# Recurrent gates in split precision, stored weight splits spread over the FFN, shared score banks, and three reorderings in a two-layer flow step

## The chip, the cores and the metric

The kernel runs on one core of one Trainium2 chip. The metric is the device time of one execution in microseconds (us): the median of the runs shown. TensorE (PE) multiplies matrices, VectorE (DVE) and ScalarE (ACT) do elementwise work, GpSimd (POOL) does a little elementwise work and issues part of the DMAs, SyncE (SP) issues most of the other DMAs. Each engine works through its own list of instructions in order.

## The reference

One inference step of two layers over 512 latent tokens and 128 context tokens, D = 1024, all in float32. Layer 0 mixes tokens by neighbourhood attention (16 heads of 64; the context tokens attend to themselves), layer 1 by a bidirectional gated linear recurrence. A SwiGLU FFN of width 2816 follows each. Every sublayer has a modulated RMS norm in front and a gated residual behind. The part that changes most, the recurrence, is cut here:

```python
def _lru_mixer(xm, h0, w_in, conv_w, conv_b, w_a, b_a, w_i, b_i, lam, w_out):
    gate, xr = jnp.split(xm @ w_in, 2, axis=-1)
    xc = _centred_depthwise_conv(xr, conv_w, conv_b)                  # width 4
    # per direction, with block-diagonal 128x128 weights (8 blocks):
    #   r = sigmoid(xc @ w_a + b_a);  i = sigmoid(xc @ w_i + b_i)
    #   a = exp(-8 r softplus(-lam)); b = sqrt(1 - a^2) * (i * xc)
    #   h_t = a_t h_{t-1} + b_t, from cached states for latent tokens
    y = (hs_f + hs_b) * jax.nn.gelu(gate)
    return y @ w_out, ...

def _swiglu(x, w_gu, w_down):
    gate, up = jnp.split(x @ w_gu, 2, axis=-1)
    return (jax.nn.silu(gate) * up) @ w_down
```

## The kernel before, in words

Everything is kept transposed: 128 features on the partitions, 640 tokens on the free axis, 8 such tiles ("KT") for D. A float32 product is done as three products of rounded parts: the operand is split into a high part (a cast to the fp32r type, on ACT) and a low part (the rest, by a subtraction on DVE), and `chunk` adds high x high, high x low and low x high for 8 tiles into one PSUM bank: 24 products of 320 or 322 columns. This is called a sum below. The split of a weight tile (`unit`, with `split` doing one ACT cast and one DVE subtraction) is done in the kernel. The recurrent gates are the exception: `gates` multiplies in full fp32, 512 and 131 columns for each gate, four gates per tile.

**Stored splits.** During the first FFN the kernel splits weights ahead of time for later stages: `keep` loads a raw tile through POOL's DMA queue, casts and subtracts it (behind the last evacuation, `mark`), and stores both parts in HBM, again through POOL's queue. Later `unit` loads both parts from there through SP's queue. `todo` lists the tiles: 16 of the recurrence's input weight "wi", 8 of its output weight "wlo", 5 of the second FFN's "gu". The raw tiles share three buffers ("mraw") with the modulation weights, whose products (`mod_cols`, "mprod") DVE does in small portions (`fill`) beside the sums.

**First FFN.** Three parts of 8, 7 and 7 hidden tiles (`ci` 0, 1, 2). For each tile j of a part come the gate and the up sums (four sums), then the part's down products (`project`, 16 sums). `keep` is called in the second and third part behind each tile, twice, up to the tile that `LATE` names, and in the first part's down products once for each output tile.

**Attention.** For each pair of heads p = 0..7 four blocks of 128 latent queries are done (`softmax`) and the prompt (`softmax_prompt`), in two halves, b0 = 0 and 2: scores on two "sp" banks, exp, a scaling by the reciprocal of the sum (one head on DVE, the other on ACT), transposes, and the products with V (`heads_out`). The output projection (`project` with `ahead`) comes behind, and its first sums can start before the last head's output is there, as far as banks are free.

**Recurrence.** `lru` runs a list `order` of steps with lags; one turn is called a lap, and there are 8, one for a tile f. On PE a lap has gates 0, 1, 2 of tile f, the sum `xa` of tile f+1 (its own bank "mx"), gate 3, then the sums `xb`, `ga` and `gb` (tags "mm", three banks in turn). `cv` (L1347, DVE) makes the convolution that the next lap's gates read. The program order of PE, DVE and ACT is held in this stage; elsewhere a planner chooses among the instructions that can run.

**Opening of the second FFN.** The recurrence's output weights are multiplied with y. Six banks (three output tiles, both halves) add up y's tiles 0 to 5, then 6, then 7; y's last tile comes late, because the last lap's scans have to end.

PSUM has eight banks: three "mm" banks that live throughout, and five that each stage lays out anew: attention tp 2, sp 2, op 1; first FFN at 2, rr 1, mx 2; recurrence mx 1 and two double banks "gp" for gates; second FFN at 1, mx 3, mc 1.

## Time and profile before

| | us |
|---|---|
| median of 3 runs | 1507.13 (1506.39 to 1509.18) |
| profiled execution | 1509.39 |
| its span in the trace | 1507.3 |
| PE busy in the span | 1477.6 (98%) |
| DVE busy | 1079.3 (72%) |
| ACT busy | 722.2 (48%) |
| POOL busy | 272.6 (18%) |

The profile is of one execution. "Busy" of PE is the time in which at least one product is under way; products overlap, so the pace of a stream is read from the distance of starts and not from the duration of one. A timeline row gives start, length, engine, line, operation and output<-inputs; a bracket at its end is how long the engine had been idle before it and what ended that. Tile names are those of the program: gp is a gate bank, xc the convolution's output, mx and mm are sum banks, whi/wlo and whx/wlx split weights.

### The profile page before, as it was taken

The page shows a single profiled execution, that of the slowest core. Times are in us where ns is not written, and L with a number is a line of the kernel's source. Part 1 is how long each engine was busy: PE and PEld are TensorE (multiplying, and loading weights), DVE is VectorE, ACT ScalarE, POOL GpSimd, SP SyncE. Part 2 cuts the span into 40 slices and gives each one's busy share as a digit, 9 for nine tenths or more (in the row PEclk, how much of TensorE's full clock was granted, in tenths as well). Part 3 has the DMA queues.
Part 4 walks back from the last instruction along what each step waited for, and adds up shares of the span by engine and source line. Part 5 has one row for each costly group of instructions (what it writes and reads, how often), then busy time and mean ns, then how long its engine had stood idle before and what let it go on. Part 6 is the DMA issues. An engine that isn't in the chain of part 4 may idle for free.

```text
span 1507.3 us, 26208 instructions
## 1 busy us (share of the span) xinstructions
PE 1477.6 (98%) x10305; PEld 1430.9 (95%) x10305; DVE 1079.3 (72%) x2034; ACT 722.2 (48%) x1336; POOL 272.6 (18%) x345
## 2 busy tenths in 40 slices
PE   7999999999999999999999999999999999999997
PEld 4999999889999999999999988899989999999997
DVE  5788887869964678888776478885875675565555
ACT  4676766664333324322443378863644342424244
POOL 0211121100100212211210001112123323222211
PEclk9999999999999999999999999999999999999999
DMA  9544645435532889886964633246332131313211
GB/s 374 170 149 148 186 148 157 124 140 181 183 126 71 304 292 327 307 271 211 324 244 138 236 126 126 71 165 225 118 124 88 67 112 57 112 57 98 71 57 70
DMA packets 83674, 246.99 MB, mean 164 GB/s; under 512 B 9264, under 2 KB 22752, under 8 KB 83424
## 3 DMA queue, kind: packets, MB, share of 16 engines
q1 hardware_dynamic: 58384, 154.97, 31.2%
q0 software_dynamic: 24848, 90.20, 17.4%
q8 instruction: 81, 1.33, 0.4%
q14 instruction: 41, 0.34, 0.1%
q10 hardware_dynamic: 320, 0.16, 0.0%
HBM read 202.02 MB, written 39.34 MB: 160 GB/s over the span
## 4 chain that ended last, share of the span: by engine, by line
PE 82%; DVE 6%; DMA 5%; issue 3%; ACT 3%; POOL 1%; SPq 0%; DVEq 0%; POOLq 0%; ACTq 0%
PE mm L246 12%; PE mm L247 12%; PE mm L245 12%; PE mx L245 4%; PE mx L247 4%; PE mx L246 4%; PE mx L1158 3%; PE mx L1159 3%; PE mx L1160 3%; PE gp L1364 2%; DMA mraw<-in_wm 2%; PE op L849 2%; PE tp L766 2%; PE mc L1158 1%; PE mc L1160 1%
## 5 line engine op out<-in xcount | busy, mean ns | idle before, releaser
L246 PE MATMUL mm<-big,whi 128*128 128x320 f32 (+2 forms) x1003 | 311.9, 311 | 2.2 <-DVE big L1470 2.2
L245 PE MATMUL mm<-big,whi 128*128 128x320 f32 (+2 forms) x1003 | 310.3, 312 | 2.3 <-ACT big L1469 1.4
L247 PE MATMUL mm<-big,wlo 128*128 128x320 f32 (+2 forms) x1003 | 311.6, 311 | 0.2 <-DVE wlo L1470 0.2
L284 DVE SCALAR_TENSOR_TENSOR mprod<-mraw,csb 128x1024 f32<-128x1024 f32 x160 | 195.6, 1223 | 19.1 <-DMA mraw<-in_wm 18.4
L246 PEld LDWEIGHTS mm<-big,whi 128*128 128x128 f32 x1003 | 189.6, 189 | 4.2 <-DVE big L1470 3.2
L245 PEld LDWEIGHTS mm<-big,whi 128*128 128x128 f32 x1003 | 188.9, 189 | 4.9 <-ACT big L1469 2.3
L247 PEld LDWEIGHTS mm<-big,wlo 128*128 128x128 f32 x1003 | 189.4, 189 | 1.6 <-DVE wlo L1470 0.4
L1469 ACT CAST whi<-raw 128x1024 fp32r<-128x1024 f32 (+2 forms) x103 | 105.5, 1025 | 152.3 <-PE mm L246 83.8
L1470 DVE TENSOR_TENSOR wlo<-raw,whi 128x1024 fp32r<-128x1024 f32 (+2 forms) x103 | 127.8, 1241 | 38.8 <-ACT whi L1469 38.3
L247 PE MATMUL mm<-big,wlx 128*128 128x320 f32 (+3 forms) x450 | 139.4, 310 | 0.0
L246 PE MATMUL mm<-big,whx 128*128 128x320 f32 (+3 forms) x450 | 139.3, 310 | 0.0
L245 PE MATMUL mm<-big,whx 128*128 128x320 f32 (+3 forms) x450 | 139.1, 309 | 0.0
L567 DVE SCALAR_TENSOR_TENSOR x<-mm,G,x 128x320 f32<-128x320 f32 (+3 forms) x207 | 83.1, 434 | 61.4 <-PE mm L247 53.6
L245 PE MATMUL mx<-big,whi 128*128 128x320 f32 (+2 forms) x325 | 101.7, 313 | 0.2 <-ACT whi L1469 0.2
L247 PE MATMUL mx<-big,wlo 128*128 128x320 f32 (+2 forms) x325 | 100.6, 310 | 0.0
L246 PE MATMUL mx<-big,whi 128*128 128x320 f32 (+2 forms) x325 | 100.5, 309 | 0.0
L280 POOL DMA_DIRECT2D mraw<-in_wm x80 | 43.2, 540 | 315.3 <-DVE mprod L284 205.4
L246 PEld LDWEIGHTS mm<-big,whx 128*128 128x128 f32 x450 | 84.9, 189 | 0.0
L247 PEld LDWEIGHTS mm<-big,wlx 128*128 128x128 f32 x450 | 84.9, 189 | 0.0
L245 PEld LDWEIGHTS mm<-big,whx 128*128 128x128 f32 x450 | 84.8, 188 | 0.0
L247 PE MATMUL mx<-big,wlx 128*128 128x320 f32 (+3 forms) x222 | 68.9, 310 | 0.0
L246 PE MATMUL mx<-big,whx 128*128 128x320 f32 (+3 forms) x222 | 68.9, 310 | 0.0
(375 smaller groups left out, 3835.9 us busy)
## 6 DMA issues: line engine op xcount, KB each, us to landing
raw<-in_gu SPq DMA_DIRECT2D x84, 512.0 KB, 3.7
mraw<-in_wm POOLq DMA_DIRECT2D x80, 512.0 KB, 4.5
raw<-in_dn SPq DMA_DIRECT2D x24, 512.0 KB, 3.6
raw<-in_wqk SPq DMA_DIRECT2D x16, 512.0 KB, 4.1
sw<-in_wm SPq DMA_DIRECT2D x16, 512.0 KB, 10.2
mraw<-in_wi POOLq DMA_DIRECT2D x16, 512.0 KB, 6.2
kwi<-kwh POOLq DMA_DIRECT2D x16, 512.0 KB, 5.7
kwi<-kwl POOLq DMA_DIRECT2D x16, 512.0 KB, 5.7
```

The lines of the kernel that those rows point to most:

```text
L245: nc.tensor.matmul(ps, hi[:, k], xhi[:, k, s], start=(k == 0), stop=False)
L246: nc.tensor.matmul(ps, hi[:, k], xlo[:, k, s], start=False, stop=False)
L247: nc.tensor.matmul(ps, lo[:, k], xhi[:, k, s], start=False, stop=(k == nk - 1))
L280: nc.gpsimd.dma_start(w, self.i["wm"][l * 6 + j - 2, f])
L284: nc.vector.scalar_tensor_tensor(prod, w, 1.0, self.csb[:, s], ALU.mult, ALU.mult, accum_out=out[:, s, f:f + 1])
L567: last = self.nc.vector.scalar_tensor_tensor(xs, ps[:, a - t0:b - t0], G[:, s, f:f + 1], xs, ALU.mult, ALU.add).ins
L766: nc.tensor.transpose(tp[:, j * P:j * P + P], s[:, j * P:j * P + P], self.ident)
L1158: nc.tensor.matmul(ps, hi[:, k], xh[:, k], start=start and k == 0, stop=False, skip_group_check=not start)
L1159: nc.tensor.matmul(ps, hi[:, k], xl[:, k], start=False, stop=False, skip_group_check=not start)
L1160: nc.tensor.matmul(ps, lo[:, k], xh[:, k], start=False, stop=(k == KH - 1), skip_group_check=not start)
L1469: high = self.nc.scalar.copy(hi, v).ins
L1470: return high, self.nc.vector.tensor_tensor(lo, v, hi.bitcast(F32), ALU.subtract).ins
```

## The change

- Gates: `keep` also splits and stores the gate weights "wg" (four tiles, two feature tiles in each). `xh` (ACT) and `xl` (DVE) split the convolution's output after `cv`. `gates` adds three products for each half of 322 columns; both halves of a gate have a bank of their own in "gp". The padded length goes from 643 to 644 so that the halves are equal. The split parts use the "raw" buffers.
- Stored splits: tables `KEEP` and `DOWN` give the number of `keep` calls behind each tile and each output tile. The list has 33 entries. In the first part the tiles 4 to 7 now have two each; the second part has 7 and 2, the third 8.
- Score banks: a pool `px` of two banks, opened before attention and closed behind the first FFN, holds "sp" in attention and "mx" in the first FFN. The first five sums of the output projection go to three "mm" and two "mx" banks.
- Last pair of heads: the prompt's softmax comes ahead of the last two blocks, and both heads are scaled on DVE.
- First gate: `xa` of tile 1 is issued before lap 0 instead of in it, on an "mm" bank; in later laps `xa` comes between gates 1 and 2 instead of between 2 and 3.
- Opening: a sum of y's tiles 0 to 6 for the fourth output tile, on the "mc" bank, comes ahead of the products with y's last tile; the loads of the last two output weights are issued behind those.
- The mask moves to a pool that is closed behind the first FFN.

```diff
-LW = 643
+LW = 644
+LH = LW // 2
-C0 = 515
+C0 = 516
-LATE = (0, 6, 7)
+KEEP = ((0, 0, 0, 0, 2, 2, 2, 2), (2, 1, 1, 1, 1, 1, 0), (2, 1, 1, 1, 1, 1, 1))
+DOWN = ((1,) * KT, (0, 0, 0, 1, 1, 0, 0, 0))
...
     def ps(self, tag=None):
         tag = tag if tag in self.ptags else self.ptags[0]
+        if self.px and tag in ("sp", "mx"):
+            return self.px.tile([P, 512], F32, tag="sp", name=self.nm(tag), bufs=2)
...
+            if name == "wg":
+                nc.gpsimd.dma_start(raw.rearrange("p (f m) -> p f m", f=2), self.i[name][2 * f:2 * f + 2].rearrange("f p w d m -> p f (w d m)"))
...
-                self.residual(f, t0, t1, self.chunk(u, hi, lo, t0, t1, not ahead or f > 1), G, nxt)
+                early = 2 * f + (t0 > 0) if ahead else KT
+                ps = self.pg(False) if early < 3 else self.ps("mx") if early < 5 else None
+                self.residual(f, t0, t1, self.chunk(u, hi, lo, t0, t1, ps=ps), G, nxt)
...
-            if a:
+            if a and p < 7:
                 nc.scalar.activation(s, s, AF.Copy, scale=rc)
...
         for b0 in (0, 2):
+            ppt = self.softmax_prompt(QS, KS, KZ, ap) if b0 and p == 7 else None
             pts = [self.softmax(p, b, QS, KS, KZ, bts, ap) for b in (b0, b0 + 1)]
...
-        todo = [("wi", KT), ("wi", 0)] + [("wi", f + g) for f in range(1, KT) for g in (KT, 0)] + [("wlo", f) for f in range(KT)]
+        todo = [k for f in range(KT) for k in [("wi", f + KT), ("wi", f)] + [("wg", f // 2)] * (1 - f % 2)] + [("wlo", f) for f in range(KT)]
...
-                if ci:
-                    self.keep(todo, 2 if j < LATE[ci] else 0)
+                self.keep(todo, KEEP[ci][j])
...
-            for ks in (range(KT - 2), (KT - 2,), (KT - 1,)):
+            for ks in (range(KT - 2), (KT - 2,)):
                 for f, c, ps in banks:
                     mm(f, c, ks, ps)
-            us += [self.unit(w[f], "m") for f in (KT - 2, KT - 1)]
             f = KT - DEH
-            ps = mm(f, 0)
+            ps = mm(f, 0, range(last), self.ps("mc")[:, 0:HT])
+            for g, c, bank in banks:
+                mm(g, c, (last,), bank)
+            us += [self.unit(w[g], "m") for g in (KT - 2, last)]
+            mm(f, 0, (last,), ps)
...
-            z["gw"] = tile([P, 2, 2, P], "gw", 2)
-            nc.sync.dma_start(z["gw"], self.i["wg"][f])
-            z["ps"] = self.chunk(z["u"], hi, lo, *CHB[0], ps=self.ps("mx")) if f else self.p0[:, 0:CHB[0][1] - CHB[0][0]]
+            z["gw"] = self.t([P, 2, 4, P], F32R, "gw", 2, lp)
+            d = self.kept["wg", f // 2].rearrange("p (h f m) -> p h f m", h=2, f=2)[:, :, f % 2]
+            nc.sync.dma_start(z["gw"].rearrange("p h g m -> p h (g m)").bitcast(F32), d)
+            z["ps"] = self.chunk(z["u"], hi, lo, *CHB[0], ps=self.ps("mx") if f > 1 else self.pg(False)) if f else self.p0[:, 0:CHB[0][1] - CHB[0][0]]
...
-                for s0, s1 in ((0, 512), (512, LW)):
-                    nc.tensor.matmul(ps[:, s0:s1], z["gw"][:, n // 2, n % 2], z["xc"][:, s0:s1], start=True, stop=True)
+                h, w = z["gw"][:, 0, n], z["gw"][:, 1, n]
+                for u, v, start, stop in ((h, z["xh"], True, False), (w, z["xh"], False, False), (h, z["xl"], False, True)):
+                    for o, a, b in ((0, 0, LH), (512, LH, LW)):
+                        nc.tensor.matmul(ps[:, o:o + b - a], u, v[:, a:b], start=start, stop=stop)
...
+        def xh(f, z):
+            z["xh"] = self.t([P, D], F32R, "raw", 3)[:, 0:LW]
+            nc.scalar.copy(z["xh"], z["xc"])
+        def xl(f, z):
+            z["xl"] = self.t([P, D], F32R, "raw", 3)[:, 0:LW]
+            nc.vector.tensor_tensor(z["xl"], z["xc"], z["xh"].bitcast(F32), ALU.subtract)
...
-        order = ((g[0], 0), (h[0], 0), (g[1], 0), (h[1], 0), (cl, 0), (e[0], 0), (e[1], 0), (g[2], 0), (xa, 1), (whole, 1), (g[3], 0), (d[0], 0),
+        order = ((g[0], 0), (h[0], 0), (g[1], 0), (h[1], 0), (cl, 0), (e[0], 0), (e[1], 0), (xa, 1), (whole, 1), (g[2], 0), (g[3], 0), (d[0], 0),
                  (h[2], 0), (sc, -1), (su, -1), (e1, 1), (xb, 1), (pad, 1), (h[3], 0), (d[1], 0), (yg, -1), (e2, 1), (egb, 0), (c1, 1),
-                 (sq, 0), (ti, 0), (hs, -1), (ga, 1), (cv, 1), (s1, 0), (bg, 1), (ls, -1), (gb, 1), (ega, 1), (ge, 0), (mu, 0))
+                 (sq, 0), (ti, 0), (hs, -1), (ga, 1), (cv, 1), (s1, 0), (bg, 1), (xh, 1), (xl, 1), (ls, -1), (gb, 1), (ega, 1), (ge, 0), (mu, 0))
...
+            if t < 0:
+                xa(1, Z[1])
+                Z[1]["v"] = self.unit(("wi", 1), "x")
```

More of the change, by code (lines that the diff above doesn't have):

```diff
@@ L143, in __init__ @@
         self.n, self.ng, self.nu, self.hold, self.late = 0, 0, 0, None, []
-        self.anchor, self.pbufs, self.lastq, self.whole, self.nraw = None, {}, {}, False, 2
+        self.anchor, self.pbufs, self.lastq, self.whole, self.nraw, self.px = None, {}, {}, False, 2, None
     def nm(self, s):
@@ L823, in attend @@
                 mid()
-            with self.tc.issue_after(self.evac) if b0 and mid else nullcontext():
-                ppt = self.softmax_prompt(QS, KS, KZ, ap) if b0 else None
+            if b0 and p < 7:
+                with self.tc.issue_after(self.evac) if mid else nullcontext():
+                    ppt = self.softmax_prompt(QS, KS, KZ, ap)
             self.heads_out(p, b0, pts, ppt, V, cv, self.ps("op"), O)
@@ L899, in ffn, with between @@
             else:
-                def between(f, n=1 - ci):
+                def between(f, n=DOWN[ci]):
                     self.fill(FG[2])
-                    self.keep(todo, n)
+                    self.keep(todo, n[f])
                 self.project(w, hhi, hlo, (l, 5), done=between)
@@ L1328, in e1 @@
             z["xr"] = tile([P, 648], "xr", 2)
-            move(z, z["ps"], CHB[0][0], ((nat(z)[:, 32:56], 320, 512, ROWS), (z["xr"][:, 517:645], 512, 640, 0)))
+            move(z, z["ps"], CHB[0][0], ((nat(z)[:, 32:56], 320, 512, ROWS), (z["xr"][:, 518:646], 512, 640, 0)))
             z["cbs"] = tile([P, 2], "cbs", 2)
@@ L1333, in pad @@
         def pad(f, z):
-            for g, a, b in ((0, 0, 2), (0, 514, 515), (1, 515, 517), (1, 645, 646)):
+            for g, a, b in ((0, 0, 2), (0, 514, 516), (1, 516, 518), (1, 646, 647)):
                 nc.scalar.mul(z["xr"][:, a:b], z["b"][:, g:g + 1].broadcast_to([P, b - a]), -1.0)
@@ L1373, in run @@
                 c = n * KT + f
-                nc.scalar.activation(z["ri"[w]][:, d], z[n][:, 0:LW], AF.Tanh, scale=0.5, bias=self.hb[:, c:c + 1])
+                o, v = [t.rearrange("p (h c) -> p h c", h=2)[:, :, 0:LH] for t in (z["ri"[w]][:, d], z[n])]
+                nc.scalar.activation(o, v, AF.Tanh, scale=0.5, bias=self.hb[:, c:c + 1])
             return run
@@ L1508, in run @@
         self.mpool = mpool.enter_context(tc.tile_pool(name="mods", bufs=1))
-        self.mask = self.t([P, 64], F32, "mask", 1)
+        self.mask = self.t([P, 64], F32, "mask", 1, self.mpool)
         nc.scalar.dma_start(self.mask, i["mask"])
@@ L1515, in run @@
         xlo = self.big()
+        shared = ExitStack()
+        self.px = shared.enter_context(tc.tile_pool(name="psx", bufs=2, space=bass.MemoryType.PSUM))
         with ExitStack() as banks:
@@ L1576, in run @@
             self.ffn(0, xhi, xlo, fp, last)
+        shared.close()
+        self.px = None
         xpool.close()
```

6 lines of the change are left out of this document (3 added, 3 removed).

## The prediction

> **What bounds the kernel now.** I read the page first, then the busy time by stage, then each engine's timeline where the change acts. The page says which engine to count:
>
> ```profile
> span 1507.3 us, 26208 instructions
> PE 1477.6 (98%) x10305; PEld 1430.9 (95%) x10305; DVE 1079.3 (72%) x2034; ACT 722.2 (48%) x1336; POOL 272.6 (18%) x345
> ```
>
> TensorE works 1477.6 of 1507.3 us, so only two things can be won: some of its 29.7 us of idle time, or TensorE work itself. The stages (window, length, then busy time of PE, PEld, DVE, ACT, POOL) show where idle time lies near the edits:
>
> ```profile
> 312.50:319.30 6.80, 4.56 (x52) 3.75 (x52) 3.15 (x15) 5.73 (x15) 0.00 (x0) 0.99 0.39 112
> 432.80:490.00 57.20, 57.20 (x390) 57.20 (x389) 26.32 (x46) 18.74 (x37) 0.00 (x0) 1.00 0.24 74
> 546.20:645.60 99.40, 99.40 (x676) 99.40 (x675) 79.13 (x135) 39.49 (x72) 23.43 (x45) 1.00 0.88 302
> 645.60:652.70 7.10, 5.99 (x39) 5.46 (x39) 5.24 (x10) 2.25 (x3) 1.28 (x3) 1.00 0.94 328
> 880.96:973.98 93.02, 93.02 (x563) 83.28 (x562) 77.58 (x115) 74.01 (x115) 11.38 (x10) 1.00 0.35 117
> ```
>
> The end of attention leaves TensorE idle 2.24 us, the step from the second gate/up part of the first FFN to its down product 1.11 us. The recurrent laps (the last row holds five, from one first gate to a later one, 18.60 us each) leave none, with DVE at 15.5 and ACT at 14.8 us a lap.
>
> **The gates.** One lap on TensorE, in order of time (start, length, line, output<-inputs). Gates 0 to 2, one sum of 24 products on the "mx" bank, gate 3, then three more sums:
>
> ```profile
> 862.36 3.56 PE L1364 MATMUL gp<-xc,gw 128*128 128x512 f32 x12 [0.97 <-issue]
> 865.90 0.30 PE L246 MATMUL mx<-big,whi 128*128 128x322 f32 x1
> 869.15 0.31 PE L247 MATMUL mx<-big,wlo 128*128 128x322 f32 x1
> 869.29 1.24 PE L1364 MATMUL gp<-xc,gw 128*128 128x512 f32 x4
> 870.52 0.31 PE L246 MATMUL mm<-big,whi 128*128 128x320 f32 x1
> 873.73 0.31 PE L247 MATMUL mm<-big,wlo 128*128 128x320 f32 x1
> 873.88 0.31 PE L245 MATMUL mm<-big,whx 128*128 128x322 f32 x1
> 877.45 0.31 PE L245 MATMUL mm<-big,whx 128*128 128x320 f32 x1
> 880.96 3.48 PE L1364 MATMUL gp<-xc,gw 128*128 128x512 f32 x12
> ```
>
> The second and the 24th product of a sum are 22 steps apart: 3.25/22 = 0.148 us a step with 322 columns, 3.21/22 = 0.146 with 320. The four sums are 24 x 0.148 = 3.55, 24 x 0.146 = 3.50, 3.57 and 3.51, together 14.13 us. The rest of the 18.60 us lap, 4.47, is the four fp32 gates with the slower first product behind each of the two groups. The change computes each gate by six split products of 322 columns. They have the form of the products around them, so I take 0.148 us: 24 x 0.148 = 3.55 a lap, a gain of 0.92, over eight laps **-7.4 us**. The other end is that the two column halves, which load the same weights one after the other, run at the duration of a weight load instead:
>
> ```profile
> L1364 PEld LDWEIGHTS gp<-xc,gw 128*128 128x128 f32 x128 | 21.6, 189 | 16.7 <-issue 16.3 <-ACT gl L1447 0.2
> ```
>
> 24 x 0.189 = 4.54 us, and nothing is won. But loads of the same length hide behind the products in the rows above, so the first value stands.
>
> **The split of the gates' input.** ACT gets a copy of 644 columns (xh), DVE a subtraction (xl), both between the convolution (cv, L1347) and the first gate. A steady lap, DVE and then ACT:
>
> ```profile
> 911.15 0.75 DVE L1325 TENSOR_TENSOR xr<-mm,r 128x64 f32<-128x64 f32 x2 [1.83 <-PE mm L247]
> 913.54 2.73 DVE L1347 SCALAR_TENSOR_TENSOR xc<-xr,cols,xc 128x643 f32<-128x643 f32 x3
> 916.18 1.49 DVE L1401 SCALAR_TENSOR_TENSOR lt<-lt,lt 128x1286 f32<-128x1286 f32 x1
> 917.59 0.82 DVE L1456 TENSOR_TENSOR big<-lt,big 128x640 fp32r<-128x640 f32 x1
> 915.69 0.71 ACT L1453 CAST big<-lt 128x640 fp32r<-128x640 f32 x1
> 916.31 0.15 ACT L1289 COPY bias<-mm 128x2 f32<-128x2 f32 x1
> 916.48 1.28 ACT L1447 ACT_TABLE_LOAD   x1
> 917.77 1.02 ACT L1447 ACTIVATE gl<-gl,bias 128x512 f32<-128x512 f32 x2
> ```
>
> The copy can start at 916.46 (cv ends at 916.27, the bias copy at 916.46) and takes what the 640-column cast takes, 0.71: 917.17. The subtraction waits for DVE's place behind L1401, 917.67, and takes 0.82 like L1456: about 918.45. In the first lap's rows DVE's xr begins 0.2 us after the sum begins that covers this chain (874.08, quoted below, against 873.88), so here that sum begins at 910.95; two sums of 3.57 and 3.51 bring the first gate to 918.03, and its four products with xh bring the first use of xl to 918.62. It is ready about 0.2 us before. Cost **0**, and up to 0.5 us in seven laps, 3.5 us, if a few semaphore steps eat that margin. Behind xl on DVE everything comes 0.74 later; the wait of 1.83 us before xr holds that even with a lap 0.92 shorter. Behind xh on ACT the Gelu comes 0.6 to 0.7 later, but the next lap's tanhs were waiting for gates, and the moved sum now stands between gate 1 and gate 2, so gate 2 doesn't wait for the tanh that frees its bank. ACT's lap grows to 15.5 us of a lap of 17.7, DVE's to 16.3.
>
> **The sum ahead of the first gate.** It fills the 0.97 us that TensorE waits before 862.36: -0.97. But it takes an "mm" bank, where it had "mx", and so shifts the ring of three by one. The order of banks becomes p0, pb0, ph0, the moved sum, pb1, pg1: pg1 now gets the bank of ph0, whose reader is egb (L1443). In lap 0:
>
> ```profile
> 874.08 0.75 DVE L1325 TENSOR_TENSOR xr<-mm,r 128x64 f32<-128x64 f32 x2 [3.58 <-PE mm L247]
> 874.67 0.48 DVE L1443 TENSOR_TENSOR gl<-mm,r 128x320 f32<-128x320 f32 x1
> 863.72 0.80 ACT L1374 ACTIVATE lt<-gp,l_hb 128x643 f32<-128x643 f32 x1 [4.19 <-PE gp L1364]
> ```
>
> egb stands on DVE behind xr, which needs the sum just before pg1. So pg1's products, which started at 873.88, would have to wait until 875.15 and a semaphore: +1.35, once. In lap 0 there is also no sum left between gates 1 and 2: gate 2 waits for the first tanh, which starts 1.36 us after its gate here, 1.13 with a gate 0.23 shorter (0.92 over four); 1.13 + 0.80 = 1.93 against two gates of 0.89: about +0.25 with the semaphore. Together **+0.6**; its ends are -0.97 (bank free in time) and +1.6. The gate weights come from the store, 512 KB instead of 256, on SP at the same place; the second lap's "wi" load goes behind the moved sum's loads on SP and isn't needed before gate 3.
>
> **The end of attention.** Idle TensorE time there:
>
> ```profile
> 312.54 0.66 PE L849 MATMUL op<-PT,big 128*64 128x128 f32 x8 [0.24 <-ACT PT L768]
> 316.57 0.66 PE L766 MATMUL tp<-ident,S 128*128 128x128 f32 x4 [0.60 <-ACT S L761]
> 318.37 0.43 PE L798 MATMUL tp<-ident,S 128*128 128x128 f32 x2 [1.14 <-DVE S L797]
> 319.26 1.55 PE L849 MATMUL op<-PT,big 128*64 128x128 f32 x12 [0.46 <-ACT PT L800]
> ```
>
> The prompt's softmax (L797, L800) is moved ahead of the last two blocks, so 1.14 + 0.46 go. The scaling behind 0.60 goes to DVE, which is busy 3.15 us where ACT is busy 5.73. With the score banks kept, two more sums of the output projection can start as soon as the last scores are read and fill what is late next, the last transposes' copies. I take **-2.0**: the 1.60 and half of the other 0.84; the ends are 0 and -2.4.
>
> **The spread of the kept splits.** The stores of split weights are 33 now, four more for the gates, each an ACT cast, a DVE subtraction and three POOL issues. Where they went before:
>
> ```profile
> 491.94 0.54 POOL L215 DMA_DIRECT2D kwi<-kwh  x1 [65.80 <-ACT kwh L212]
> L213 DVE TENSOR_TENSOR kwl<-mraw,kwh 128x1024 fp32r<-128x1024 f32 x29 | 35.5, 1223 | 17.7 <-DMA kwi<-kwl 7.5 <-ACT kwh L212 4.3 <-DMA kwlo<-kwl 4.3
> ```
>
> POOL's queue stood 65.8 us behind a store whose cast was due only at the first down product, while DVE was at 46% (26.32 of 57.20). Eight stores now fall there: 8 x 1.22 = 9.8 us of DVE beside 30.9 us that it is idle. The second part gets 7 stores instead of 12, and the window before the gap (DVE 79.13 of 99.40, DMA 0.88) is lightened by 6.1 us of DVE. So the gap at 645.60 should go: **-1.1**. Queued behind the earlier casts are the mod products and the evacuations, with TensorE's sums behind those; the other end is that the gap only moves and comes up three times, +3.3. The four extra splits, 4.9 us of DVE, are hidden by the same idle time.
>
> **The last products.** TensorE waits once for the last y:
>
> ```profile
> 1016.33 0.41 PE L255 MATMUL mm<-big,whi 128*128 128x320 f32 x1 [0.45 <-DVE big L1456]
> ```
>
> A sum of 21 products (3.1 us) on the "mc" bank now stands ahead: **-0.45** (other end 0). The loads of the last two output weights are issued behind the same products, still two whole sums (7 us) ahead of their use. The mask's pool and the 644th column cost nothing: a 644th of ACT and DVE work that isn't the bound.
>
> **Sum**: -7.4 + 0 + 0.6 - 2.0 - 1.1 - 0.45 = -10.3 us. The profiled execution took 1509.39 us for its span of 1507.3; it would come to 1499.1. The median of the runs, 1507.13, is 2.3 us below it, so the forecast for the median is **1496.8 us**.
>
> **Rivals.** (1) *The split is late.* xl misses its place by about 0.5 us in each steady lap, because the margin of 0.2 was counted without semaphores: 1496.8 + 3.5 = 1500.3. For it: the thin margin; against: DVE's place behind L1401 is known to a tenth. (2) *The kept splits disturb the first part.* The gap doesn't go but moves to the earlier stores and comes three times: 1496.8 + 1.1 + 3.3 = 1501.2. Against it: DVE's 30.9 us of idle time. (3) *The gates don't get faster*, with weight loads of 0.189 as the pace: 1496.8 + 7.4 = 1504.2 with the laps' 0.07 us more each, 1504.8. (4) *The lap turns from TensorE's into a chain's*, the one that ends slower: copy and subtraction stand in series in the loop from gate to tanh to xr to cv to gate, and nothing of them is hidden: 18.60 + 0.71 + 0.82 = 20.13 a lap, 2.45 above the forecast lap, in seven laps 17.2: 1514. It decides once the chain from xr to xl is over the 7.7 us that the two covering sums and four gate products give; I counted 7.5. Against it: TensorE isn't idle in 93.02 us of laps, and DVE waits 1.83 us for it in each.
>
> (5) *ScalarE becomes the lap's bound*, by a pause behind each change of its function tables, of which a lap has three:
>
> ```profile
> L1385 ACT ACT_TABLE_LOAD x8 | 10.3, 1283 | 0.1
> L1395 ACT ACT_TABLE_LOAD x8 | 10.3, 1283 | 0.1
> L1447 ACT ACT_TABLE_LOAD x8 | 10.3, 1283 | 0.1
> ```
>
> A pause as long as the load would make ACT's lap 15.5 + 3 x 1.28 = 19.3 us, 1.7 above the forecast lap, and the time 1496.8 + 7 x 1.7 = 1508.7. Against it: the ACTIVATE at 917.77 starts 0.01 us after its load ends. The Trainium skill (ScalarE: Activation LUTs, "What ACT_TABLE_LOAD costs") has such a pause, a drain of 1.38 us behind every load of 1.28; by that rule the estimate would be 15.5 + 4.1 = 19.6 us a lap and 1510. The load agrees with the trace, the drain doesn't, and the measurement decides.
>
> **How the numbers follow.** Forecast with its own ends (1494 to 1499.5): 0.62. Rival 1: 0.14; rival 2: 0.08; rival 3: 0.06; rival 4: 0.05; rival 5: 0.01; something outside these, such as another order of work chosen around the edits, 0.04, spread over both sides. The range holds the forecast with its ends and rivals 1 and 2, and leaves out the other 0.16: 1493 to 1503. A difference of 0.2% (3 us) is about what this kernel's runs can tell from no change. Faster: 0.62 + 0.14 + 0.08 + 0.02 = 0.86; same: rivals 3 and 5 and 0.01, 0.08; slower: rival 4 and 0.01, 0.06.
>
> **What would show it.** Right: laps of about 17.7 us with no TensorE wait on xl; 12 and 12 gate products of 0.148 steps; one wait of about 1.3 us of "mm" for L1443 in lap 0 and none before the first gate; no wait for L797 and L800; DVE above 60% at 432 to 490 and no gap at 645; no wait at the last y. Wrong: laps above 18.2, or waits in front of the gates' last two products in every lap; gaps of a microsecond in the first FFN; TensorE still idle 2 us where attention ends.

## The result and the profile after

The changed kernel takes 1497.76 us (median of 5 runs, 1495.96 to 1500.60), against 1509.18 (1506.39 to 1511.93, 5 runs) of the kernel before beside it: a ratio of 0.9928, 95% interval 0.9909 to 0.9947. The forecast was 1496.8, range 1493 to 1503. The profiled execution of the changed kernel took 1496.28 us. Its page:

```profile
span 1493.9 us, 26401 instructions
PE 1467.3 (98%) x10369; PEld 1438.2 (96%) x10369; DVE 1087.8 (73%) x2050; ACT 730.4 (49%) x1344; POOL 280.7 (19%) x357
```

PE is busy 10.3 us less than before (some of it in the start, see experiment 12), and its idle time went from 29.7 us to 26.6. To see where the 13.4 us of span went, I cut both traces at four marks that all kernels here share: the select products ("tp") of the opening, the norm statistics ("at") behind attention, the column products ("gp" from "ones") ahead of the recurrence, and the statistics behind the opening of the second FFN. Timeline of PE, before:

```profile
41.61 0.61 PE L419 MATMUL tp<-sel,big 128*128 128x2 f32 x4 [0.49 <-ACT big L412]
376.24 1.39 PE L493 MATMUL at<-ones,ssq 128*128 128x1 f32 x12
854.80 1.28 PE L514 MATMUL gp<-gl,ones 128*128 128x128 f32 x10
1038.42 0.72 PE L493 MATMUL at<-ones,ssq 128*128 128x1 f32 x6
```

The same marks after:

```profile
38.95 0.61 PE L426 MATMUL tp<-sel,big 128*128 128x2 f32 x4 [0.49 <-ACT big L419]
371.12 1.40 PE L500 MATMUL at<-ones,ssq 128*128 128x1 f32 x12
848.79 1.28 PE L521 MATMUL gp<-gl,ones 128*128 128x128 f32 x10
1024.20 0.72 PE L500 MATMUL at<-ones,ssq 128*128 128x1 f32 x6
```

| stage, by marks | before | after | difference | forecast |
|---|---|---|---|---|
| start | 41.61 | 38.95 | -2.66 | 0 |
| attention | 334.63 | 332.17 | -2.46 | -2.0 |
| first FFN | 478.56 | 477.67 | -0.89 | -1.1 |
| recurrence and opening of the second FFN | 183.62 | 175.41 | -8.21 | -7.25 |
| rest | 468.88 | 469.70 | +0.82 | 0 |

How far a stage of one execution can be trusted is seen from kernels that leave it alone. The recurrence stage of the changed kernel came to 175.40 to 175.46 in five executions (this one, the repeat, and three kernels below whose edits lie elsewhere); differences of 0.1 us count there. The start came anywhere between 38.95 and 42.53, attention (eight kernels with the change's own code there, this one and the repeat) between 329.6 and 334.2, so those single differences are not exact. The rest came between 468.6 and 471.4 (without experiment 3), so its +0.82 says nothing.

Part of attention's scatter is TensorE's clock. The traces hold stretches of 3.41 us at a granted clock of 0.5, each of which can cost up to 1.7 us. Attention has two of them in the profile of the kernel before (from 295.2 and 319.1 us), one in the changed kernel's (from 324.0), and none to two in the other nine. The first FFN has none before and one after (from 375.2); in experiment 11, which has none there, it takes 476.48, and in eight executions with the change's FFN and one such stretch 477.66 to 478.22. So up to 1.7 of attention's -2.46 is the clock's, and the first FFN's -0.89 is too small by up to as much.

The stretches shown before, after the change (window, length, busy time of PE, PEld, DVE, ACT, POOL; the second row is moved by the 5.12 us by which the mark behind attention comes earlier, the last row holds four laps):

```profile
432.80:490.00 57.20, 57.20 (x389) 57.20 (x389) 40.98 (x66) 24.10 (x42) 12.01 (x23) 1.00 0.77 270
541.08:640.48 99.40, 99.40 (x676) 99.40 (x675) 88.41 (x152) 40.07 (x71) 24.83 (x47) 1.00 0.91 323
891.35:962.13 70.78, 70.78 (x483) 70.78 (x482) 65.13 (x97) 60.93 (x97) 8.96 (x8) 1.00 0.40 135
```

DVE's work in the first part of the FFN rose from 26.32 to 40.98 us, as forecast for the moved stores. In the second row it rose as well, from 79.13 to 88.41, where the forecast had it fall by 6.1. Laps are 17.70 us long, with DVE at 16.28 and ACT at 15.23 (forecast 17.7, 16.3 and 15.5). And of PE's waits between the end of attention and the opening of the second FFN (320 to 1014 us; total, count, longest) one is left:

```profile
PE mm L252 <- ACT big L1496: 1.6, 1, 1.6
```

Short pauses, as the 0.30 of lap 0 and the 0.4 of lap 1 below, don't show in this list.

Gates 0 and 1 of laps 0, 1, 2 and 6, on PE (lap 0's row holds all four gates):

```profile
858.77 4.02 PE L1379 MATMUL gp<-raw,gw 128*128 128x322 f32 x24
873.23 2.31 PE L1379 MATMUL gp<-raw,gw 128*128 128x322 f32 x12
891.35 1.92 PE L1379 MATMUL gp<-raw,gw 128*128 128x322 f32 x12
962.13 1.92 PE L1379 MATMUL gp<-raw,gw 128*128 128x322 f32 x12
```

Starts of laps are 14.46 us apart for lap 0 (its sum stands ahead of it now), 18.12 for lap 1, then 17.70 on average. Lap 1's twelve products take 2.31 instead of 1.92: xl came 0.4 us late there, once.

### The profile page after: what moved, and what is told of

It reads as the page before. It is cut to its first block, busy times and chain, and to the rows that moved or that the text cites. A ratio compares the mean times of both kernels' runs of the same rounds, so it can differ in the third digit from the quotient of the medians.

```text
span 1493.9 us, 26401 instructions
## 1 busy us (share of the span) xinstructions
PE 1467.3 (98%) x10369; PEld 1438.2 (96%) x10369; DVE 1087.8 (73%) x2050; ACT 730.4 (49%) x1344; POOL 280.7 (19%) x357
## 5 line engine op out<-in xcount | busy, mean ns | idle before, releaser
L253 PE MATMUL mm<-big,whi 128*128 128x320 f32 (+3 forms) x1010 | 313.9, 311 | 1.9 <-DVE big L1497 1.9
L252 PE MATMUL mm<-big,whi 128*128 128x320 f32 (+3 forms) x1010 | 312.1, 311 | 3.2 <-ACT big L1496 2.1
L254 PE MATMUL mm<-big,wlo 128*128 128x320 f32 (+3 forms) x1010 | 313.7, 311 | 0.2 <-DVE wlo L1497 0.2
L291 DVE SCALAR_TENSOR_TENSOR mprod<-mraw,csb 128x1024 f32<-128x1024 f32 x160 | 195.9, 1224 | 19.2 <-DMA mraw<-in_wm 18.4
L253 PE MATMUL mm<-big,whx 128*128 128x320 f32 (+3 forms) x443 | 137.4, 310 | 0.0
L252 PE MATMUL mm<-big,whx 128*128 128x320 f32 (+3 forms) x443 | 136.8, 310 | 0.0
L254 PE MATMUL mx<-big,wlo 128*128 128x320 f32 (+3 forms) x318 | 99.2, 312 | 0.0
L253 PE MATMUL mx<-big,whi 128*128 128x320 f32 (+3 forms) x318 | 99.0, 311 | 0.0
L252 PE MATMUL mx<-big,whi 128*128 128x320 f32 (+3 forms) x318 | 98.7, 311 | 0.0
```

What stands on the lines that cost most here:

```text
L252: nc.tensor.matmul(ps, hi[:, k], xhi[:, k, s], start=(k == 0), stop=False)
L253: nc.tensor.matmul(ps, hi[:, k], xlo[:, k, s], start=False, stop=False)
L254: nc.tensor.matmul(ps, lo[:, k], xhi[:, k, s], start=False, stop=(k == nk - 1))
L291: nc.vector.scalar_tensor_tensor(prod, w, 1.0, self.csb[:, s], ALU.mult, ALU.mult, accum_out=out[:, s, f:f + 1])
```

## The experiments

Each kernel is the changed one with the edit shown, except the second, which is the kernel before. Where the text compares stages, they are cut at the marks above.

**1. Everything but the gates.** The gate weights are loaded unsplit, and their four stores are left out.

```diff
-                h, w = z["gw"][:, 0, n], z["gw"][:, 1, n]
-                for u, v, start, stop in ((h, z["xh"], True, False), (w, z["xh"], False, False), (h, z["xl"], False, True)):
-                    for o, a, b in ((0, 0, LH), (512, LH, LW)):
-                        nc.tensor.matmul(ps[:, o:o + b - a], u, v[:, a:b], start=start, stop=stop)
+                for o, a, b in ((0, 0, LH), (512, LH, LW)):
+                    nc.tensor.matmul(ps[:, o:o + b - a], z["gw"][:, n // 2, n % 2], z["xc"][:, a:b], start=True, stop=True)
...
-                 ... (bg, 1), (xh, 1), (xl, 1), (ls, -1), ...
+                 ... (bg, 1), (ls, -1), ...
```

> The changed kernel with its gates in full fp32 again, from the unsplit weights: no copy and subtraction of the convolution's output, no stored gate weights; all else of the change stays. If the split products are what gained, the laps go back from 17.7 to 18.6 us and the time rises by 7.4 us, to about 1505. If the gain lies in the reorderings and the spread of the stores, the laps may grow but the time stays within 2 us of 1497.8.

Measured: 1503.68 us, ratio to before 0.9967 (0.9953 to 0.9981), so 0.0039 or 5.9 us worse than the changed kernel. The recurrence stage is 181.47, 6.06 longer. Gates 0 and 1 of lap 1:

```profile
876.30 2.33 PE L1376 MATMUL gp<-xc,gw 128*128 128x322 f32 x8
```

Lap 6 starts at 968.82, so a lap is 18.50: full-precision gates in even halves and in the new order are only 0.07 a lap cheaper than those of the kernel before (18.58), and the split products give the other 0.81. The gates' gain needs the split products; it is 5.9 to 6.1 us here and not the 7.4 that was expected.

**2. The gates alone, in the kernel before.** The edits to `gates`, `xh`, `xl`, the stored gate weights, the length and the mask's pool, nothing else.

> The kernel before with the split gates alone: the stores follow the old tables (with four more entries), the order of the laps, the banks, the prompt and the opening are as before. If the reordering of the laps is needed to collect the gain, two waits show: about 2.5 us in front of the first gate (0.97 and the copy and subtraction, 0.73 + 0.83), and in each lap about 0.4 us in front of gate 2, whose bank the first tanh holds until 2.1 us after the lap's start while two gates take 1.8. Then the laps are 18.1 and the time is -7.4 + 1.5 + 3.2 = -2.7 us from before, about 1505. If the gates bring their gain alone, the laps are 17.7 and the time is 7 us below before.

Measured: 1510.26 us, ratio to before 1.0008 (0.9997 to 1.0018): nothing. The recurrence stage is 183.84, where it was 183.62. Its waits on PE:

```profile
863.48 3.48 PE L1371 MATMUL gp<-raw,gw 128*128 128x322 f32 x18 [1.76 <-ACT raw L1376]
883.96 1.15 PE L1371 MATMUL gp<-raw,gw 128*128 128x322 f32 x6 [0.18 <-ACT lt L1390]
1014.51 0.41 PE L258 MATMUL mm<-big,whi 128*128 128x320 f32 x1 [1.24 <-ACT big L1469]
1015.38 0.45 PE L259 MATMUL mm<-big,whi 128*128 128x320 f32 x1 [0.45 <-DVE big L1472]
```

The first gate waits for the new split (1.76, was 0.97); gate 2 waits in each lap for a tanh that the faster gates have outrun, so laps are 18.17 and not 17.7; and the last y, which the shorter laps make later against PE, costs 1.69 instead of 0.45, with a stretch at half clock behind it (from 1015.6). This last wait was not in the expectation of -2.7 us. Part by part the two halves of the change give about 2 us (experiment 1 in this stage: 181.47 against 183.62) and nothing; together they give 8.2. The reorderings are what lets the gates' saving through.

**3. Gate 2 back in front of the sum, in every lap.**

```diff
-        order = (... (e[1], 0), (xa, 1), (whole, 1), (g[2], 0), (g[3], 0), (d[0], 0),
+        order = (... (e[1], 0), (g[2], 0), (xa, 1), (whole, 1), (g[3], 0), (d[0], 0),
```

> The changed kernel with gate 2 ahead of the moved sum again, as in the laps before; the sum ahead of the first gate stays. If gate 2 waits for the tanh that frees its bank, each of the laps 1 to 6 grows from 17.7 to about 18.1, and the span by 2.4 us. If the order of gate 2 doesn't matter, the laps stay at 17.7.

Measured: laps of 18.17 us, the recurrence stage 178.25 (+2.84). One of the six waits:

```profile
894.88 1.15 PE L1379 MATMUL gp<-raw,gw 128*128 128x322 f32 x6 [0.22 <-ACT lt L1398]
```

A recorded wait of 0.22 lengthens the lap by 0.48. About 0.26 of the difference is in how waits are recorded: the last product's modelled length is 0.31 where the stream's step is 0.148, so the first 0.16 of a pause isn't counted, and the first product behind a pause takes 0.41 instead of 0.31. (The time, 1503.60 in one run, is also raised by a wait of 2.2 us in the second FFN that neither theory had: its sum on "mc" waited for L1182, and a stretch at half clock follows.)

**4. The sum back in lap 0, on its own bank.** One load moves along with it.

```diff
-            z["ps"] = self.chunk(..., ps=self.ps("mx") if f > 1 else self.pg(False)) if f else ...
+            z["ps"] = self.chunk(..., ps=self.ps("mx")) if f else ...
...
-                if 0 <= t + lag < KT and (t or step is not xa):
+                if 0 <= t + lag < KT:
...
-                xa(1, Z[1])
```

> The changed kernel with the second tile's sum back in lap 0, on its own bank instead of one of the three. If the changed kernel pays nothing for the bank, the undoing costs what stood in front of the first gate: TensorE waits there for the convolution, copy and subtraction, about 2.2 us, gate 2 of lap 0 no longer waits 0.3, so the stage from the first gate to the opening ends about 1.9 us later. By the forecast's reckoning, with 1.35 us paid for the bank in lap 0, it would end only 0.6 us later.

Measured: the recurrence stage is 177.08, +1.67, with the wait ahead of the first gate:

```profile
859.36 2.33 PE L1380 MATMUL gp<-raw,gw 128*128 128x322 f32 x12 [1.74 <-ACT raw L1385]
```

With the split the gap is 1.74 us and not the 0.97 of the kernel before: xh stands in it too. The stage's +1.67 is near the 1.9 of the first theory and far from the 0.6 of the forecast's reckoning: nothing was paid for the bank.

**5. The old places of the kept splits.**

```diff
-KEEP = ((0, 0, 0, 0, 2, 2, 2, 2), (2, 1, 1, 1, 1, 1, 0), (2, 1, 1, 1, 1, 1, 1))
-DOWN = ((1,) * KT, (0, 0, 0, 1, 1, 0, 0, 0))
+KEEP = ((0,) * KT, (2, 2, 2, 2, 2, 2, 0), (2, 2, 2, 2, 2, 2, 2))
+DOWN = ((1,) * KT, (0,) * KT)
```

> The changed kernel with the stores of the split weights where the old tables had them: none at the first part's tiles, one at each of its output tiles, two at each tile but the last of the second part, the other 13 in the third. If the spread removed the gap, TensorE stands about 1.1 us between the second part's gate and up sums and its down products, POOL's queue waits some 60 us for one cast in the first part, and the time rises by 1.1 us. If the gap was chance, no wait of TensorE over 0.3 us shows in the first FFN.

Measured: 1501.44 us, ratio to before 0.9940 (0.9924 to 0.9955): 0.0012 worse than the changed kernel's, with intervals that overlap. In the profiled execution the first FFN is 483.65 long, 6.0 more, and the gap is this one:

```profile
648.50 0.47 PE L252 MATMUL mm<-big,whi 128*128 128x320 f32 x1 [4.12 <-ACT big L1496]
```

The cast that it waits for stood on ScalarE behind a kept split's cast (L219), and that one waited for the store of the split before it, since "kwh" is one buffer:

```profile
647.04 1.04 ACT L219 CAST kwh<-mraw 128x1024 fp32r<-128x1024 f32 x1 [5.13 <-DMA kwi<-kwh]
648.00 0.45 ACT L1496 CAST big<-sg 128x320 fp32r<-128x320 f32 x1
```

In the kernel before the kept cast at this place waited 4.15 us for a store, with the gap of 1.1 behind it. POOL's queue waited 56.8 us for one cast in the first part, as expected.

Behind the gap TensorE ran at about half its clock (window, length, busy time of PE to POOL, then the granted clock):

```profile
648.50:652.00 3.50, 3.50 (x14) 3.50 (x15) 3.50 (x6) 0.79 (x1) 0.41 (x1) 0.53 0.83 335
```

14 products where 3.5/0.148 = 23.6 fit: 1.4 us more. The gap that the spread removes is 1.1 us in the profile of the kernel before and 4.1 in this one; its worth lies between 0.9 and 6: 1.8 by the ratios to before, 3.7 by the medians.

**6. The score banks given back, the output projection's first sums on three banks.** The pool `px` is not opened.

```diff
-                early = 2 * f + (t0 > 0) if ahead else KT
-                ps = self.pg(False) if early < 3 else self.ps("mx") if early < 5 else None
-                self.residual(f, t0, t1, self.chunk(u, hi, lo, t0, t1, ps=ps), G, nxt)
+                self.residual(f, t0, t1, self.chunk(u, hi, lo, t0, t1, not ahead or f > 1), G, nxt)
```

> The changed kernel without the shared score banks: attention and the first FFN lay out their own, and the output projection's first four sums are on the three mm banks as before. If the two extra sums fill TensorE where attention ends, its idle time between the last scores and the projection rises by 2 us or more over the changed kernel's 1.6. If the prompt's place alone brought the gain, the idle time stays at about 1.6.

Measured: attention 335.83 long, 3.66 more. Most of that can be the clock: 3.41 us from 295.5 and 6.83 from 319.4 ran at half clock, against 3.41 us in all in the changed kernel. PE at its end:

```profile
318.53 0.63 PE L773 MATMUL tp<-ident,S 128*128 128x128 f32 x4 [1.29 <-DVE S L770]
319.72 1.09 PE L773 MATMUL tp<-ident,S 128*128 128x128 f32 x4 [0.56 <-DVE S L770]
321.48 1.12 PE L858 MATMUL op<-PT,big 128*64 128x128 f32 x8 [0.68 <-ACT PT L775]
```

The prompt's wait is gone, and the last two blocks' scaling (L770) waits longer in its place: 2.53 us of idle time, about as much as before the change (2.44) and 0.9 more than the changed kernel's 1.64. That is between the two expectations.

**7. The prompt's softmax last again, the banks kept.**

```diff
-            if a and p < 7:
+            if a:
...
-            ppt = self.softmax_prompt(QS, KS, KZ, ap) if b0 and p == 7 else None
+            ppt = None
...
-            if b0 and p < 7:
+            if b0:
```

> The changed kernel with the last pair's prompt softmax behind the last blocks and one head's scaling on ACT again; the shared banks stay. If the prompt's chain was the wait, about 1.6 us of TensorE waits on the prompt's scaling and copy come back. If the two extra sums are what fills that time, no wait on the prompt shows and the end of attention is as long as in the changed kernel.

Measured: 1497.84 us in one run, attention 333.33. PE at its end:

```profile
315.03 0.66 PE L775 MATMUL tp<-ident,S 128*128 128x128 f32 x4 [0.60 <-ACT S L770]
315.87 0.42 PE L252 MATMUL mx<-big,whi 128*128 128x320 f32 x1 [0.18 <-ACT S L802]
326.30 0.72 PE L252 MATMUL mm<-big,whi 128*128 128x320 f32 x3 [1.61 <-ACT big L1496]
```

No wait of 1.14 for the prompt: the sums on the two extra banks fill it. What ends last is the same with and without the prompt's move, the cast of the last pair's output, 1.64 us in the changed kernel. But with 0.24 at 310.99 the idle time is 2.63 us, no less than without the banks. The length of the part that the edit touches says the same. It runs from the last pair's first score minimum ("nm") to the mark behind attention; its start before, after, and here:

```profile
300.23 0.08 DVE L754 DVE_READ_ACCUMULATOR2_ANT nm<- 128x1 f32 x1
296.21 0.08 DVE L763 DVE_READ_ACCUMULATOR2_ANT nm<- 128x1 f32 x1
298.70 0.08 DVE L763 DVE_READ_ACCUMULATOR2_ANT nm<- 128x1 f32 x1
```

That makes 76.01, 74.91 and 74.53 us (76.20 in experiment 6). The first two hold a stretch of 3.41 us at half clock, this one none, experiment 6 one of 6.83. In the eight kernels with the change's attention and no such stretch here (experiments 1, 3, 4, 5, 8, 9, 10 and 12) it takes 73.23 to 73.36. So at equal clock this edit costs 1.2 us even with the banks kept, and the whole change at this place is worth 1.1. The idle time is 2.44 before, 2.53 and 2.63 with one half of the change, and 1.64 with both: each half needs the other. What the prompt's place and the scaling on DVE do apart was not tried.

**8. The old opening of the second FFN.**

```diff
-            for ks in (range(KT - 2), (KT - 2,)):
+            for ks in (range(KT - 2), (KT - 2,), (KT - 1,)):
...
+            us += [self.unit(w[f], "m") for f in (KT - 2, KT - 1)]
...
-            ps = mm(f, 0, range(last), self.ps("mc")[:, 0:HT])
-            for g, c, bank in banks:
-                mm(g, c, (last,), bank)
-            us += [self.unit(w[g], "m") for g in (KT - 2, last)]
-            mm(f, 0, (last,), ps)
+            ps = mm(f, 0)
```

> The changed kernel with the opening's order of before: no sum on the mc bank ahead of the products with y's last tile. If the chain of the last lap (22.5 us from its first gate to its last split) is longer than the work ahead of it (about 22.1 us with the faster gates), TensorE waits there 0.5 to 1.5 us. If faster gates also shorten the chain, it doesn't wait.

Measured: the recurrence stage is 179.17, +3.76. PE at the last y:

```profile
1005.17 0.41 PE L261 MATMUL mm<-big,whi 128*128 128x320 f32 x1 [1.25 <-ACT big L1474]
1006.03 0.42 PE L262 MATMUL mm<-big,whi 128*128 128x320 f32 x1 [0.45 <-DVE big L1477]
```

These are 1.70 us. The rest is the clock, in the windows over the wait and behind it:

```profile
1003.60:1007.00 3.40, 1.70 (x10) 1.20 (x9) 1.88 (x3) 0.73 (x1) 0.60 (x1) 1.00 1.03 400
1007.00:1010.50 3.50, 3.50 (x17) 3.50 (x16) 3.50 (x11) 2.35 (x5) 2.51 (x5) 0.56 1.00 328
```

In the kernel before the same place, with a wait of 0.45 alone, kept its clock:

```profile
1013.00:1016.40 3.40, 2.95 (x19) 2.50 (x18) 2.38 (x4) 0.73 (x1) 1.38 (x2) 1.00 1.03 403
1016.40:1019.80 3.40, 3.40 (x23) 3.40 (x24) 2.80 (x8) 1.88 (x4) 1.92 (x4) 1.00 1.06 384
```

From 1007.50 to 1010.71 the products start 0.267 us apart instead of 0.148, twelve times, and with the steps at both ends that is about 1.5 us. (The 17 of the window count those that only reach into it.) The two waits' unrecorded parts are some 0.5, which makes 3.7 of the 3.76.

**9. The low part later on VectorE.**

```diff
-                 ... (xh, 1), (xl, 1), (ls, -1), (gb, 1), (ega, 1), (ge, 0), (mu, 0))
+                 ... (xh, 1), (ls, -1), (gb, 1), (ega, 1), (xl, 1), (ge, 0), (mu, 0))
```

> The copy of the low part of the gates' state (xl) is put behind ls and the early half's egb and ega work, about 0.74 + 0.40 us later on VectorE in each lap. Theory (the low part is on the lap's path with a margin of only about 0.2 us): TensorE waits some 0.9 us in each steady lap in front of the six products that read it, laps of about 18.6 us instead of 17.7, some +6.5 us over the changed kernel. Rival (the margin is wider than the rows make it, since the other four products of a step can run first): laps stay at 17.7 and the time is that of the changed kernel within 0.2%.

Measured: 1501.88 us, ratio to before 0.9958 (0.9941 to 0.9974); the recurrence stage 181.71, +6.30. Lap 2 and the start of lap 3:

```profile
892.26 0.74 PE L1379 MATMUL gp<-raw,gw 128*128 128x322 f32 x4
893.85 1.45 PE L1379 MATMUL gp<-raw,gw 128*128 128x322 f32 x8 [0.84 <-DVE raw L1388]
911.11 0.74 PE L1379 MATMUL gp<-raw,gw 128*128 128x322 f32 x4
```

A wait of 0.84 in the place that was foretold, behind the four products with xh, and laps of 18.84. Counted from its lap's first gate, xl ends 1.53 us in, where it ended 0.38 in: 1.15 later, and the lap is 1.14 longer. The margin of 0.2 took its part off the wait, but the step from DVE to PE (0.05) and the slower first product (0.1) put nearly as much back. By the medians the time is 4.1 us above the changed kernel's and not 6.3; attention was 2.5 us shorter in this profile.

**10. The low part earlier.**

```diff
-                 ... (cv, 1), (s1, 0), (bg, 1), (xh, 1), (xl, 1), (ls, -1), ...
+                 ... (cv, 1), (bg, 1), (xh, 1), (xl, 1), (s1, 0), (ls, -1), ...
```

> The copy of the low part goes ahead of the sum of states s1 on VectorE. Theory: lap 1's single wait of 0.4 us for the low part goes, the steady laps stay at 17.7, time 0 to 0.5 us below the changed kernel. Rival: VectorE now waits about 0.9 us for ScalarE's high part with s1 queued behind it, and what follows s1 is late: laps up to 17.8 and more, +0.7 us or more.

Measured: the recurrence stage is 174.84, -0.57. Lap 1 and lap 2:

```profile
878.13 1.92 PE L1379 MATMUL gp<-raw,gw 128*128 128x322 f32 x12
895.81 1.92 PE L1379 MATMUL gp<-raw,gw 128*128 128x322 f32 x12
```

Lap 1's products no longer wait (1.92 where they took 2.31), and the lap is 17.68. It is better than the changed kernel by 0.04%, which the times can't show (1499.13 in one run); it is the one improvement found.

**11. The three "mm" banks strictly in turn.**

```diff
-        return self.psum.tile([P, 512], F32, tag="mm", name=self.nm("mm"), bufs=3)
...
+        self.nmm += 1
+        return self.psum.tile([P, 512], F32, tag=f"mm{self.nmm % 3}", name=self.nm("mm"), bufs=1)
```

> The three banks of the mm tiles become three tags of one bank each, handed out in turn. Theory (the forecast wait of lap 0 was right in its mechanism and only the order in which the pool hands out banks was not): the third gate tile of lap 0 waits about 1.35 us for VectorE's egb product, once, and the time is some 1.3 us above the changed kernel. Rival (the bank is free in any order): no such wait, the time within 0.2% of the changed kernel.

Measured: the recurrence stage is 176.39, +0.98, with the wait that the changed kernel doesn't have, on VectorE's egb (here L1469, from 868.37 to 868.84):

```profile
868.89 0.42 PE L254 MATMUL mm<-big,whx 128*128 128x322 f32 x1 [1.14 <-DVE gl L1469]
```

Lap 0 is 1.39 longer for it (15.85 against 14.46). Lap 1 is 0.45 shorter (17.67 against 18.12), since xl is no longer late there.

**12. The changed kernel again.**

> The changed kernel once more, nothing edited. Theory (the 2.7 us that the profiled executions differ in their first 42 us are the moment at which the TensorE clock comes up, and no part of the change): the second select of tp starts anywhere between 38.5 and 42 us, and the laps are 17.7 as before. Rival (it is a part of the change): the select starts at 38.95 us again within 0.2 us.

Measured: 1497.50 us in one run. The select of the start:

```profile
39.59 0.61 PE L426 MATMUL tp<-sel,big 128*128 128x2 f32 x4 [0.49 <-ACT big L419]
```

0.64 later than in the first execution of the same code, outside the 0.2 that the rival allowed. Together with the other kernels, which leave the start alone and lie between 39.59 and 42.53, this makes it a spread between executions, of which the change's profile had the lucky end. The time is lost between 12 and 18 us, where the same two products take about twice as long before as after:

```profile
15.79 2.05 PE L467 MATMUL op<-big,ones 128*128 128x512 f32 x2
14.51 1.10 PE L474 MATMUL op<-big,ones 128*128 128x512 f32 x2
```

The trace's record of the granted clock begins, at full speed, at 18.8 us before, at 13.4 after and at 14.1 in the repeat; nothing is recorded ahead of that. In the seven executions in which it begins between 12.9 and 14.1 us, the select starts at 38.95 to 40.02; in the seven in which it begins between 18.4 and 21.4, at 41.25 to 42.53. So the theory holds: what differs is the moment at which the clock comes up.

## Why the prediction was right, point by point

**The gates: right.** Six laps, from the first gate of lap 0 to that of lap 6, took 111.46 us before (862.36 to 973.82) and take 103.36 now, with one sum (3.55) moved out: 4.55 won, where six times 0.92 less 0.30 for gate 2 in lap 0 and 0.4 for lap 1 makes 4.8. The rest is a reading: the prediction's row of five laps ended at 973.98, 0.16 behind the first gate, so a lap was 18.58 and not 18.60, and a steady lap wins 0.88. From lap 6 to the mark behind it 2.53 us are won (two laps' gates and the 0.45 of the last y make 2.29). The rival pace of 0.189 is out: weight loads are that long and hidden, and twelve gate products take 1.92 where steps of 0.189 would make it 2.39.

**The split of the gates' input: right, and as narrow as forecast.** A steady lap (lap 2), DVE's sum of states and xl, and ACT's xh:

```profile
889.50 1.49 DVE L1425 SCALAR_TENSOR_TENSOR lt<-lt,lt 128x1288 f32<-128x1288 f32 x1
889.69 0.74 ACT L1384 CAST raw<-xc 128x644 fp32r<-128x644 f32 x1
890.91 0.82 DVE L1388 TENSOR_TENSOR raw<-xc,raw 128x644 fp32r<-128x644 f32 x1
```

xl is ready at 891.73; its first reader would start at 891.35 + 4 x 0.148 = 891.94. Rivals 1 and 4 fall with the laps of 17.70; experiment 9 shows what a late xl costs in each lap. Lap 1 alone missed the margin, by 0.4, inside the 0.5 that was allowed. Rival 5 is out as well: ACT has 15.23 us of work in a lap of 17.70, and nothing waits for a pause behind a table load. The Trainium skill (ScalarE: Activation LUTs, "What ACT_TABLE_LOAD costs") has a drain of about 1.38 us with each load. The trace doesn't agree: in the same lap the ACTIVATE behind a load starts 0.01 us after its end (891.74 after 891.73).

**The sum ahead of the first gate: two terms right, one wrong.** The gap of 0.97 went (1.13 with its unrecorded part), and gate 2 waited 0.30 in lap 0 (forecast 0.25): the 24 products take 3.85 us, from 858.77 to 862.62, where 24 x 0.148 are 3.55. The failed step is the ring: "pg1 now gets the bank of ph0" and its +1.35. The rows of the changed kernel are the third gate sum's first product and egb, which still reads ph0 after that:

```profile
866.14 0.31 PE L252 MATMUL mm<-big,whx 128*128 128x322 f32 x1
866.93 0.49 DVE L1467 TENSOR_TENSOR gl<-mm,r 128x320 f32<-128x320 f32 x1
```

So pg1 has another bank. "In turn" was my reading of the pool, and it isn't its rule. Experiment 11 puts the banks in turn and gets the wait, 1.14 us and a lap 0 longer by 1.39: the mechanism and its size were right, the order of banks was not. The 0.98 that it costs the stage is as much as the 0.96 us by which the recurrence came out better than its sum.

**The end of attention: size near by luck, reason wrong.** Forecast -2.0, found -2.46 in an execution pair, but with about 2 us of scatter to both sides and up to 1.7 of it from one stretch fewer at half clock. At equal clock the place is worth 1.1 (experiment 7). The failed step is the sum of 1.60 and half of 0.84: of 2.44 us of recorded idle time only 0.8 went, because a wait of 1.64 for the cast of the last pair's output, which I had not named, took the place of the others. The prompt's move alone only shifts the wait (experiment 6), and the banks alone leave as much idle time as before (experiment 7).

**The spread of the kept splits: direction right, reason wrong, size uncertain.** The gap at 645 is gone and no new one came, so rival 2 is out. But DVE was not lightened there: it is busy 88.41 of 99.40 us instead of 79.13, because products for the modulation moved in ("mprod", 40.02 us instead of 28.50). TensorE stood for a cast on ScalarE, behind a kept cast that waited for a store (experiment 5). The gap was priced by one execution, -1.1 (found -0.89, with a stretch at half clock against it); experiment 5 shows that the same gap can cost 6.

**The last products: right only in sign.** I priced the wait as it stood, 0.45. With laps 0.9 us shorter the last scans are later against PE, and the wait would have been 1.70 with a slow clock behind it: left out of the change it costs 3.76. The sum came out right because the moved sum covers this too.

The total agrees better than its terms, and the median better than the gain. The profiled pair differs by 13.1 us, of which 2.66 are the start's spread. By the runs' medians it is 11.4, against 10.3 forecast; the missing wait of the ring explains 1.0 of that. That the median came within 1.0 us of the forecast is luck in part: the kernel before, run beside the change, took 1509.18, 2.05 more than the 1507.13 that the forecast was counted from, and the larger gain made up for half of it.

## What to carry to other kernels

A shorter stage pays only as far as everything behind it was waiting for TensorE alone: price the faster loop once with the old order (the first entry, the place where it outruns its own consumer, the last exit), since here the gates alone gave nothing and 8.2 us with three moved sums. Count an existing wait as it will be once the rest of the change is in, not as it stands. And don't derive waits from an assumed order of buffers: what bank a tile has can be read from who still uses it.

## What was not expected of the hardware

Light stretches of TensorE work cost twice. In 3.4 us over the last y of experiment 8 TensorE was busy 1.70 and the next 3.5 us ran at a granted clock of 0.56; in the kernel before, busy 2.95 of 3.4, the clock stayed at 1.00. In all 14 traces, the end of the kernel left out, the slow stretches run at half clock and are 3.41 us long (one is 6.83), and they start whole multiples of 3.413 us after the first entry of the clock's record. On that grid the changed kernel has this pair at the end of attention:

```profile
320.60:324.01 3.41, 1.77 (x17) 1.42 (x13) 1.58 (x5) 0.94 (x2) 1.62 (x3) 1.00 0.58 171
324.01:327.43 3.42, 3.42 (x15) 3.42 (x14) 3.29 (x8) 3.05 (x5) 0.00 (x0) 0.50 0.72 290
```

In the repeat the same wait of 1.63 us falls on two such windows, which are busy 3.10 and 2.09 us, and the clock stays at 1.00. So whether a pause costs a slow stretch is also chance. Over all traces, 17 windows ahead of a slow stretch were busy 0.21 to 1.84 us; five windows busy 1.56 to 1.80 kept the clock, and so did every one above 1.84, save two kinds. One lay in a slow stretch itself (experiment 6, 2.45); the others, one in each of eleven executions, hold most of the 24 products of one column at the mark behind attention and count as fully busy.

The Trainium skill (TensorE: Matmul & The Clock Gate, "Why this matters for your kernels") warns of idle gaps above about 3 us. Here a gap of 1.25 and one of 0.45 close together did it, so the measurement asks for more care than the page.
